# A joint mask selector, pair products in blocks of 64 tokens, and expert 0's tokens picked by one-hot matmuls

## The chip, the cores and the metric

One Trainium2 chip, one of its cores. The metric is the device time of one execution in microseconds. Three executions of the kernel before took 1454.84, 1455.51 and 1457.64 us (median 1455.51).

## The reference, cut to what matters

Two transformer blocks run one after the other on 512 tokens of width 1024, all in fp32. The change touches three places of them.

```
# first block, SSD mixer: a_cs are cumulative sums within chunks of 128 tokens
seg = a_cs[..., :, None] - a_cs[..., None, :]
lmat = exp(where(causal, seg, -inf))                       # 12 heads, 4 chunks
y_diag = einsum('bcgls,bcghls,bcsghp->bclghp', cb, lmat, xdt)

# second block, HGRN2 mixer: b is the running sum of log f within a chunk of 64 tokens
diff = b[:, :, :, None, :] - b[:, :, None, :, :]
decay = where(causal, exp(minimum(diff, 0)), 0)
scores = einsum('bhtk,bhtsk,bhsk->bhts', qc, decay, kc)    # 4 heads, 128 channels k
o_intra = einsum('bhts,bhsv->bhtv', scores, vc)

# second block, mixture of experts: top group, then top 2 of its 4 experts
for e in range(16):
    h = silu(t @ w_gate[e]) * (t @ w_up[e])                # 1024 -> 512
    y = y + gates[:, e:e + 1] * (h @ w_down[e])            # 512 -> 1024
```

## The kernel before, in words

All tokens stay on one core, in four tiles of 128 tokens. A dense product with weights is made with fp32 precision out of three matmuls of rounded operands: `split` (L265) lets ScalarE copy a weight unit to `whi` (L270) and VectorE subtract that from the raw weights into `wlo` (L271), and `mm3` (L274) issues hi times hi (L276), hi times lo (L277 or L278) and lo times hi. A plain fp32 matmul shows as two matmul records in the trace (28 groups of 4 matmuls at L1416 are 224 records). Weights come in units of 512 KB through SyncE's DMA queue (L212) into a ring of raw buffers; `fill` loads and splits ahead. Which engine subtracts a unit, and behind which instruction, is written in `s.plan` and `s.fence`. The order of each engine's instructions is set by a list scheduler from priorities; `issue_after` adds a dependence and `ahead` moves priority. Side work such as the mixers runs as generators between the dense matmuls of a neighbouring stage and shares TensorE with them.

**SSD masks.** For each of 16 units (4 chunks times 4 groups) `ssd_mask_unit` (L830) fills one PSUM bank: the causal mask (L840), the cumulative sums of three heads broadcast to all rows by a selector column, once for their high parts (L841) and once for their low parts (L842), both with 48 rows of the array, and the product of B and C (L843). ScalarE takes the exponential (L846), VectorE multiplies (L847).

**HGRN2 pair products.** `hgrn_head` (L1375) makes the scores of a head as a sum over eight groups. The diagonal is k times q masked by the identity (L1393, L1394). For each level l from 6 down to 0 the tokens are cut into blocks of 2 times 2^l, the left half of each block scaled as keys and the right half as queries (L1407 to L1412, exponential on ScalarE at L1409), and four matmuls of 128 by 128 (L1416), one for each token tile, give all pairs; VectorE copies those of this level under a mask into `PT` (L1417). Thus a head has 32 matmuls, all heads 128, or 256 records.

**Entry to the experts.** `moe` projects the mixers' output with `w_out_2`, and for each token tile `after` adds the residual (L403), transposes the tile (L2023), computes the router's logits (L2028), the rank of each token within its expert (`route_tile`, `ranks`, L1731 to L1733), and a one-hot matrix of expert 0's 96 slots (L2049). The normed tokens go to a DRAM tensor `xnd`. When the last tile is ranked, `slots_row` (L1829) turns the one-hot matrix into token numbers (`sn_v`, `sn_i`), and POOL gathers 96 rows of `xnd` with an indirect DMA (L1874). `expert_pick` transposes the rows (L1887), and `put_split` (L315) makes `ex_xh` and `ex_xl`, on which expert 0's first matmul waits. Expert 1 is fetched in the same way right behind. Two of the weight splits of this stretch are on POOL (L271). A DMA of SyncE (`mark`, L2116) stands ahead of the next weight loads; the final norm's gain is broadcast by TensorE (L125). After that each expert has 4 units of gate weights, 4 of up weights and 4 of down weights, and the tokens of expert e+1 are picked while expert e is computed.

Of the kernel before, what the change touches and what calls it, by code (L numbers as in the profile page):

```python
# [7 lines left out]
F32 = mybir.dt.float32  # L8
# [62 lines left out]
class Kern:  # L71
# [202 lines left out]
    def mm3(s, ps, a, asl, b, bsl, first, last):  # L274
# [3 lines left out]
        mm(ps, a.lo[asl], b.hi[bsl], start=False, stop=last)  # L278
# [99 lines left out]
    def projR(s, src, ld, nk, get, x, after, tail=3, mid=None, lag=2, order=None):  # L378
# [4 lines left out]
        for half in range(2):  # L383
            cs = slice(half * 512, half * 512 + 512)
# [16 lines left out]
            for tt in range(NT):  # L401
                mms(ws, tt)
                nc.vector.tensor_add(x[:, tt, cs], x[:, tt, cs], pss[tt])  # L403
# [372 lines left out]
    def ssd_dt(s, pd, x):  # L776
# [38 lines left out]
        s.ssd_sel = pd.tile([48, 16], F32R, name="ssd_sel")  # L815
        V.tensor_add(s.ssd_sel, eq[:, 3], eq[:, 2])
        hm = pd.tile([48, 3], F32, name="ssd_hm")
        V.tensor_reduce(hm, eq[:, 0:3], AX.X, OP.add)
        yield
        pt = s.ptr.tile([P, 512], F32, name="tr")  # L820
        nc.tensor.transpose(pt[:48, 0:P], cs[:, 0].rearrange("p a b -> p (a b)"), s.ident)
        hl = s.tmp.tile([48, 2, P], F32R, name="ssd_hl", tag="h")
        hi, lo = hl[:, 0], hl[:, 1]
        s.put_split(pt[:48, 0:P], hi, lo)
        s.ssd_cs = Split(*(pd.tile([48, 3, P], F32R, name="ssd_c" + i) for i in ("H", "L")))
        sh = [48, 3, P]
        for o, v in ((s.ssd_cs.hi, hi), (s.ssd_cs.lo, lo)):
            V.tensor_mul(o, v.bitcast(F32)[:, None, :].to_broadcast(sh), hm[:, :, None].to_broadcast(sh))
        yield

    def ssd_mask_unit(s, pl, c, g):
# [7 lines left out]
        sel = s.ssd_sel[:, u:u + 1].to_broadcast([48, P])  # L839
# [506 lines left out]
    def hgrn_consts(s, pool):  # L1346
# [30 lines left out]
    def hgrn_head(s, pt, h, fq, PT, kd, qx, el):  # L1377
# [950 lines left out]
```

## Time and profile before

| | |
|---|---|
| profiled execution, its own time | 1453.98 us |
| its span | 1452.2 us |
| mean granted TensorE clock | 0.987 |
| busy: TensorE, VectorE, ScalarE, POOL | 96%, 67%, 54%, 7% |
| chain that ended last, share of TensorE | 86% |
| stretch 1110 to 1120 us: TensorE busy | 8.89 of 10 us |
| stretch 1150 to 1160 us: TensorE busy | 10.0 of 10 us |

The time of an execution is a little above the span of its profile. "Busy" of TensorE counts modelled ends of pipelined matmuls, so that distances from one start to the next say more of its pace than durations. The first block's mixer lies around 60 to 260 us, the second block's around 800 to 1060, its projection up to 1119, and the experts from there to the end.

### The profile page before, as it was taken

Reading aid. Unit: us, or ns where it says so; the run is one execution under the profiler, and the core shown is the slowest. Engines: PE = TensorE matmul, PEld = TensorE weight load, DVE = VectorE, ACT = ScalarE, POOL = GpSimd, SP = SyncE. Lnnn points to the kernel's source line nnn. Section 1 sums busy time; section 2 is a strip of 40 time slices with the busy share of each in tenths; the row PEclk is TensorE's granted clock in tenths of the full one; section 3 lists DMA queues with packets and bytes.
Section 4 is the critical chain, followed back from the end, with each engine's and each line's share of the span. In section 5 each row is a group of like instructions: output and inputs, shape, how many; then the busy total and the mean of one; then the engine's idle time right before and its main releaser. Section 6 shows DMA issues by size and latency. Waiting matters only on the chain.

```text
span 1452.2 us, 20178 instructions
## 1 busy us (share of the span) xinstructions
PE 1399.7 (96%) x7467; PEld 1130.2 (78%) x7467; DVE 977.7 (67%) x1772; ACT 779.2 (54%) x1200; POOL 103.8 (7%) x103
## 2 busy tenths in 40 slices
PE   7999999999999999999999999999998599999996
PEld 6888887787879888888888889877887367777774
DVE  6989577565465444444365997766555599999997
ACT  6465654434334333233344685554443388888885
POOL 1000000010010000000000400000102111111111
PEclk9999999999999999999999999999999699999998
DMA  7353342521223333323232423120754899999993
GB/s 199 92 136 112 90 131 73 174 88 58 75 71 116 102 95 94 101 88 100 89 101 87 134 74 88 41 77 18 260 204 172 226 357 356 353 343 349 349 349 130
DMA packets 145933, 223.51 MB, mean 154 GB/s; under 512 B 18466, under 2 KB 71106, under 8 KB 145816
## 3 DMA queue, kind: packets, MB, share of 16 engines
q1 hardware_dynamic: 136852, 200.48, 42.7%
q0 software_dynamic: 3568, 10.34, 3.0%
q10 hardware_dynamic: 5412, 11.37, 2.2%
q8 instruction: 59, 0.97, 0.3%
q14 instruction: 42, 0.34, 0.1%
HBM read 208.41 MB, written 14.95 MB: 154 GB/s over the span
## 4 chain that ended last, share of the span: by engine, by line
PE 86%; DVE 6%; ACT 3%; DMA 2%; issue 2%; POOL 1%; DVEq 0%; SPq 0%; ACTq 0%; POOLq 0%
PE mm L276 24%; PE mm L278 24%; PE mm L277 24%; PE sm L1416 2%; PE tr L1548 1%; PE tr L323 1%; PE tr L1887 1%; PE sm L1532 1%; POOL rs_r L291 1%; DMA ex_g<-xnd,sn_i 1%; DVE wlo L271 1%; PE sm L879 1%; PE sm L276 1%; PE tr L1540 1%; PE sm L2028 1%
## 5 line engine op out<-in xcount | busy, mean ns | idle before, releaser
L271 DVE TENSOR_TENSOR wlo<-raw,whi 128x1024 fp32r<-128x1024 f32 (+1 forms) x351 | 423.6, 1222 | 216.4 <-ACT whi L270 213.5
L270 ACT ACTIVATE whi<-raw 128x1024 fp32r<-128x1024 f32 (+1 forms) x356 | 372.7, 1057 | 293.2 <-PE mm L277 154.0
L276 PE MATMUL mm<-hT_hi,whi 128*128 128x512 f32 (+1 forms) x768 | 283.2, 369 | 1.9 <-DVE x L403 1.7
L278 PE MATMUL mm<-hT_hi,wlo 128*128 128x512 f32 (+1 forms) x768 | 281.5, 367 | 0.0
L277 PE MATMUL mm<-hT_lo,whi 128*128 128x512 f32 (+1 forms) x768 | 280.9, 366 | 0.0
L276 PE MATMUL mm<-whi,hT_hi 128*128 128x512 f32 (+1 forms) x592 | 219.7, 371 | 1.4 <-ACT hT_hi L315 1.4
L278 PE MATMUL mm<-whi,hT_lo 128*128 128x512 f32 (+1 forms) x592 | 217.9, 368 | 0.0
L277 PE MATMUL mm<-wlo,hT_hi 128*128 128x512 f32 (+1 forms) x592 | 217.0, 367 | 0.0
L278 PEld LDWEIGHTS mm<-hT_hi,wlo 128*128 128x128 f32 x768 | 144.7, 188 | 24.3
L276 PEld LDWEIGHTS mm<-hT_hi,whi 128*128 128x128 f32 x768 | 144.3, 188 | 24.8 <-DVE x L403 1.9
L277 PEld LDWEIGHTS mm<-hT_lo,whi 128*128 128x128 f32 x768 | 144.6, 188 | 23.3
L276 PEld LDWEIGHTS mm<-whi,hT_hi 128*128 128x128 f32 x592 | 111.8, 189 | 20.7 <-ACT hT_hi L315 2.3
L278 PEld LDWEIGHTS mm<-whi,hT_lo 128*128 128x128 f32 x592 | 111.7, 189 | 19.2 <-issue 0.6
L277 PEld LDWEIGHTS mm<-wlo,hT_hi 128*128 128x128 f32 x592 | 112.0, 189 | 18.5 <-issue 1.0
L276 PE MATMUL mm<-whi,ex_xh 128*96 128x512 f32 x256 | 102.8, 402 | 1.3 <-ACT ex_xh L315 0.6
L291 POOL TENSOR_TENSOR rs_r<-rs_v,mhalf 128x1 f32<-128x1 f32 (+2 forms) x42 | 33.4, 798 | 980.2 <-DVE rs_v L289 823.9
L277 PE MATMUL mm<-wlo,ex_xh 128*96 128x512 f32 x256 | 101.4, 396 | 0.0
L278 PE MATMUL mm<-whi,ex_xl 128*96 128x512 f32 x256 | 100.9, 395 | 0.0
L276 PEld LDWEIGHTS mm<-whi,ex_xh 128*96 128x96 f32 x256 | 41.5, 162 | 19.0 <-ACT ex_xh L315 1.1
L278 PEld LDWEIGHTS mm<-whi,ex_xl 128*96 128x96 f32 x256 | 41.6, 162 | 18.1
L277 PEld LDWEIGHTS mm<-wlo,ex_xh 128*96 128x96 f32 x256 | 41.8, 163 | 16.9
L1246 DVE SCALAR_TENSOR_TENSOR cv<-mm,cols,cv 128x511 f32<-128x511 f32 (+1 forms) x44 | 33.0, 749 | 30.0 <-ACT cv L1243 29.2
(568 smaller groups left out, 2060.3 us busy)
## 6 DMA issues: line engine op xcount, KB each, us to landing
raw<-in_w_gate SPq DMA_DIRECT2D x64, 512.0 KB
raw<-in_w_up SPq DMA_DIRECT2D x64, 512.0 KB
raw<-in_w_down SPq DMA_DIRECT2D x64, 512.0 KB
raw<-in_ffn_w_up SPq DMA_DIRECT2D x44, 512.0 KB
raw<-in_w_in SPq DMA_DIRECT2D x40, 512.0 KB
raw<-in_ffn_w_down SPq DMA_DIRECT2D x22, 512.0 KB
raw<-in_w_out SPq DMA_DIRECT2D x16, 512.0 KB
raw<-in_w_in SPq DMA_DIRECT2D x8, 520.0 KB
```

The source lines that it names most:

```text
L270: s.hi_op = s.nc.scalar.activation(hv, v, AF.Copy).ins
L271: eng.tensor_sub(lv, v, hv.bitcast(F32))
L276: mm(ps, a.hi[asl], b.hi[bsl], start=first, stop=False)
L277: mm(ps, a.hi[asl], b.lo[bsl], start=False, stop=False)
L278: mm(ps, a.lo[asl], b.hi[bsl], start=False, stop=last)
L291: s.pow_op = nc.gpsimd.tensor_tensor(r, v, s.mhalf[:, :n], OP.pow).ins
L323: nc.tensor.transpose(ps[:, i * P:(i + 1) * P], src[:, (k0 + i) * P:(k0 + i + 1) * P], s.ident)
L879: nc.tensor.matmul(yd[:, o:o + 64], L[:, j], xdt[:, h], start=True, stop=True)
L1246: V.scalar_tensor_tensor(y[:, d:], ps[:, :512 - d], cw[:, w:w + 1], y[:, d:], op0=OP.mult, op1=OP.add)
L1416: nc.tensor.matmul(ps[:, sl], qk[:, sl], qk[:, sl], start=True, stop=True)
L1532: nc.tensor.matmul(ps[:, :n], qa[:, h, sl], ka[:, h, :n], start=True, stop=False)
L1540: nc.tensor.transpose(pt[:, j * P:j * P + P], p[:, j * P:j * P + P], s.ident)
```

## The change

Three parts of the program are changed.

1. The high and low parts of the cumulative sums are stacked into 128 rows (0 to 47 and 64 to 111, the rest zero by the selector), so that one matmul with 128 rows (L848) takes the place of the two with 48 rows.
2. The pair products are made for blocks of 64 tokens. Diagonal and levels 5 to 0 take eight matmuls of 64 by 64 each, whose outputs lie in PSUM partitions 0 to 63 and 64 to 127 in turn, that is in the two column halves of the array (L1413); level 6 takes four, in the lower half alone (L1442). Two levels share a PSUM bank. VectorE's masked copies are half as long (256 elements) and go into a new tile `PC`; three ScalarE copies per head bring level 6 and the blocks into `PT`. A head has 60 matmuls in 4 steps of TensorE instead of 32 in 8.
3. Expert 0's tokens are not gathered. `first` multiplies each token tile (stationary) by its one-hot matrix, now in fp32 (L2063, 8 matmuls per tile); ScalarE and VectorE read the two PSUM banks and apply the norm's gain (L2164 to L2167). Expert 1 alone is gathered, with its one-hot matrix made per tile and its pick placed after the third up unit. The two POOL splits go to VectorE, behind the residual adds; the `mark` DMA is gone; the final gain comes by a POOL DMA of 128 by 1024 instead of two broadcast matmuls.

```diff
 def ssd_mask_unit
-        nc.tensor.matmul(o, sel, s.ssd_cs.hi.rearrange("p j t -> p (j t)"), start=False, stop=False)
-        nc.tensor.matmul(o, sel, s.ssd_cs.lo.rearrange("p j t -> p (j t)"), start=False, stop=True)
+        nc.tensor.matmul(o, s.ssd_sel[:, u:u + 1].to_broadcast([P, P]), s.ssd_cs.rearrange("p j t -> p (j t)"),
+                         start=False, stop=True)
 def hgrn_head
+        PC = pt.tile([P, NT, 64], F32, name="hg_PC", bufs=2)
+        def blocks(ps, c0, a, b_):
+            for tt in range(NT):
+                for i in range(2):
+                    c = tt * P + i * 64
+                    nc.tensor.matmul(ps[i * 64:i * 64 + 64, c0 + tt * 64:c0 + tt * 64 + 64], a[:, c:c + 64],
+                                     b_[:, c:c + 64], start=True, stop=True)
...
-                nc.tensor.matmul(ps[:, sl], qk[:, sl], qk[:, sl], start=True, stop=True)
-            V.copy_predicated(PT[:, h], s.hg_mask[l][:, None, :].to_broadcast([P, NT, P]),
-                              ps.rearrange("p (a b) -> p a b", a=NT))
+            if l == 6:
+                blocks(ps, 0, k, q)
+                for tt in range(NT):
+                    nc.tensor.matmul(ps[0:64, 256 + tt * 64:320 + tt * 64], qk[:, tt * P:tt * P + 64],
+                                     qk[:, tt * P + 64:tt * P + P], start=True, stop=True)
+                V.tensor_mul(PC, pv[:, 0], s.hg_id[:, None, :].to_broadcast([P, NT, 64]))
+                nc.scalar.activation(PT[0:64, h, :, 64:], pv[0:64, 1], AF.Copy)
+            else:
+                for i, (_, v) in enumerate(qks):
+                    blocks(ps, i * 256, v, v)
+                for i, (n, _) in enumerate(qks):
+                    V.copy_predicated(PC, s.hg_mask[n][:, None, :].to_broadcast([P, NT, 64]), pv[:, i])
+        for i in range(2):
+            r = slice(i * 64, i * 64 + 64)
+            nc.scalar.activation(PT[r, h, :, r], PC[r], AF.Copy)
 def moe
+        def first(tt):
+            for b in range(2):
+                for k in range(4):
+                    c = (4 * b + k) * P
+                    nc.tensor.matmul(p0[b][:, k * CAP:(k + 1) * CAP], x[:, tt, c:c + P], oh[0][:, tt],
+                                     start=tt == 0 and k == 0, stop=tt == 3 and k == 3)
...
-            V.tensor_scalar(oh[:, tt], s.slot, s.rk[:, tt, 0:1], None, op0=OP.is_equal)
+            for e in range(2):
+                V.tensor_scalar(oh[e][:, tt], s.slot, s.rk[:, tt, e:e + 1], None, op0=OP.is_equal)
...
-        s.plan = [(nc.gpsimd, []), (nc.gpsimd, [s.pow_op])]
+        s.plan = [(V, [s.add_ops[0]]), (V, [s.add_ops[1]])]
...
-            gf = s.bcast_pe(s.gain, grow, "gain")
-        with s.tc.issue_after(nc.sync.dma_start(mark, ix[0]).ins):
-            s.fill()
-        xT = s.expert_pick(pe, xgs[0])
+        xT = s.expert_xT(pe)
+        for k in range(KD):
+            ps = p0[k // 4][:, k % 4 * CAP:k % 4 * CAP + CAP]
+            gk = s.cols2[:, 96 + k:97 + k]
+            nc.scalar.activation(xT.hi[:, k], ps, AF.Copy, scale=gk)
+            V.scalar_tensor_tensor(xT.lo[:, k], ps, gk, xT.hi[:, k].bitcast(F32), op0=OP.mult, op1=OP.subtract)
...
-            xT = s.expert_pick(pe, xgs[(e + 1) % XG])
+            with s.tc.issue_after(s.gate_op) if e == 0 else nullcontext():
+                xT = s.expert_pick(pe, xgs[(e + 1) % XG])
```

The scheduler moves instructions with it. TensorE in the second block's mixer, first head: L276 to L278 are dense matmuls of the projection, `sm` is a PSUM bank of the pair products. Before, a group of eight:

```order
L278 MATMUL mm<-hT_hi,wlo 128x512
L276 MATMUL mm<-hT_hi,whi 128x512
L277 MATMUL mm<-hT_lo,whi 128x512
L1416 MATMUL sm<-hg_qk 128x128 x8
L278 MATMUL mm<-hT_hi,wlo 128x512
```

and now, from level 6 of the first head on:

```order
L276 MATMUL mm<-hT_hi,whi 128x512
L1442 MATMUL sm<-hg_qk 64x64 x4
L277 MATMUL mm<-hT_lo,whi 128x512
L1413 MATMUL sm<-hg_qk 64x64 x8
L278 MATMUL mm<-hT_hi,wlo 128x512
L276 MATMUL mm<-hT_hi,whi 128x512
L1413 MATMUL sm<-hg_qk 64x64 x8
L277 MATMUL mm<-hT_lo,whi 128x512
L278 MATMUL mm<-hT_hi,wlo 128x512
```

The 64 by 64 matmuls stand in 33 runs in all, with full-width matmuls between them, down to runs of one in the second head.

TensorE at the entry to the experts: `tr` and `sm` with `rt_` names are the router, L2063 are the one-hot matmuls, and the rows with `ex_xh` are expert 0's gate. Before:

```order
L1748 LDWEIGHTS rt_o
L1748 MATMUL sm<-rt_Mb,rt_o 128x16
L125 MATMUL mm<-grow,ones 128x512 x2
L1887 MATMUL tr<-ident,ex_g_9992 128x96 x8
L276 MATMUL mm<-whi,ex_xh 96x512
L277 MATMUL mm<-wlo,ex_xh 96x512
```

and now, from the last dense matmul of the projection up to the last logits, and then up to the gate:

```order
L278 MATMUL mm<-whi,hT_lo 128x512
L2063 MATMUL mm<-rt_oh_9582,x 128x96 x15
L2071 MATMUL tr<-ident,x 128x128 x4
L2063 MATMUL mm<-rt_oh_9582,x 128x96
L2076 MATMUL sm<-rt_w,rt_h 128x20 x4
```

```order
L1785 MATMUL sm<-rt_Mb,rt_o 128x16
L2063 MATMUL mm<-rt_oh_9582,x 128x96 x8
L1871 LDWEIGHTS rt_oh_9583
L1871 MATMUL sm<-rt_tb,rt_oh_9583 96x2
L276 MATMUL mm<-whi,ex_xh 96x512
L277 MATMUL mm<-wlo,ex_xh 96x512
```

The gather's transposes and the broadcast are gone from here; the one-hot matmuls of tiles 0 and 1 fill TensorE behind the projection, those of tile 3 (L2063 x8) stand right ahead of the gate, and the pick of expert 1 stands behind the third up unit.

VectorE at the same place now has the low parts of expert 0's tokens (`ex_xl`) between route work and weight splits:

```order
L2167 SCALAR_TENSOR_TENSOR ex_xl<-mm,cols_2799,ex_xh 128x96 x2
L1805 TENSOR_TENSOR rt_w<-rt_w,rt_se 128x4
L1834 TENSOR_REDUCE rt_rk_10279<-rt_x 128x4
L2167 SCALAR_TENSOR_TENSOR ex_xl<-mm,cols_2799,ex_xh 128x96 x2
L1806 RECIPROCAL rt_w<-rt_w 128x4
L1833 TENSOR_TENSOR rt_x<-rt_M,rt_rk 128x64
L1807 TENSOR_TENSOR rt_w<-rt_w,rt_e_10253 128x4
L271 TENSOR_TENSOR wlo<-raw,whi 128x1024
```

Route work that stood alone while the gather was under way now shares the queue with what expert 0 waits for.

## Rows read from the trace of the kernel before

**Rows 1.** Page: the chain that ended last, share of the span by engine.

```profile
PE 86%; DVE 6%; ACT 3%; DMA 2%; issue 2%; POOL 1%; DVEq 0%; SPq 0%; ACTq 0%; POOLq 0%
```

**Rows 2.** Windows: length, busy us of PE, PEld, DVE, ACT, POOL; PEclk, DMA share, GB/s.

```profile
200.00:230.00 30.00, 30.00 (x195) 25.36 (x194) 23.60 (x43) 14.91 (x36) 1.10 (x2) 1.00 0.34 105
830.00:890.00 60.00, 60.00 (x419) 55.04 (x418) 51.29 (x106) 51.71 (x70) 0.00 (x0) 1.00 0.31 89
1120.00:1130.00 10.00, 3.70 (x26) 3.18 (x27) 8.47 (x43) 3.69 (x6) 3.25 (x3) 0.61 0.89 315
1130.00:1140.00 10.00, 4.07 (x12) 1.43 (x10) 5.21 (x24) 2.51 (x5) 3.42 (x3) 0.50 0.84 81
1200.00:1300.00 100.00, 100.00 (x480) 71.11 (x479) 92.45 (x92) 85.92 (x103) 14.16 (x12) 1.00 1.04 353
```

**Rows 3.** Timeline of PE, 16 pair-product records: start us, us to last end.

```profile
835.45 0.40 PE L277 MATMUL mm<-hT_lo,whi 128*128 128x512 f32 x1
835.68 1.95 PE L1416 MATMUL sm<-hg_qk 128*128 128x128 f32 x16
837.38 0.47 PE L278 MATMUL mm<-hT_hi,wlo 128*128 128x512 f32 x1
837.70 0.39 PE L276 MATMUL mm<-hT_hi,whi 128*128 128x512 f32 x1
```

**Rows 4.** Timeline of PE, one SSD mask unit.

```profile
173.75 0.33 PE L840 MATMUL sm<-neg_lt,identb 128*128 128x384 bf16 x1
...
174.28 0.34 PE L842 MATMUL sm<-ssd_cL,ssd_sel 48*128 48x384 f32 x1
174.55 0.49 PE L843 MATMUL sm<-CT,BT 128*128 128x128 f32 x2
174.79 0.36 PE L276 MATMUL mm<-memT_hi,whi 128*128 128x256 f32 x1
```

**Rows 5.** Timeline of PE, four records on 64 rows of the array between dense matmuls.

```profile
58.55 0.40 PE L278 MATMUL mm<-hT_hi,wlo 128*128 128x512 f32 x1
58.88 0.49 PE L597 MATMUL sm<-s_oo,s_bre 64*128 64x128 f32 x4
...
59.64 0.40 PE L277 MATMUL mm<-hT_lo,whi 128*128 128x512 f32 x1
```

**Rows 6.** Timeline of PE, 64 by 64 matmuls of the S5 mixer in column halves.

```profile
105.63 0.40 PE L278 MATMUL mm<-hT_hi,wlo 128*128 128x512 f32 x1
105.95 2.09 PE L686 MATMUL sm<-s_U,s_I 128*64 128x64 f32 x64
107.97 0.66 PE L695 MATMUL sm<-s_U,s_T 128*128 128x64 f32 x4
```

**Rows 7.** Chain of waits at the entry to the experts: start us, us, what.

```profile
1117.49 0.80 PE sm L2028 x8
...
1118.70 1.75 DVE rt_oh L2049
...
1122.77 1.90 PE sm L2028 x8
...
1124.87 1.32 DVE rs_t L301
...
1129.00 0.18 DVE rt_oh L2049
...
1130.83 14.23 DMA ex_g<-xnd,sn_i
...
1146.64 0.73 PE mm L276
```

**Rows 8.** Timeline of POOL at the same place, two weight splits.

```profile
1118.03 2.35 POOL L271 TENSOR_TENSOR wlo<-raw,whi 128x1024 fp32r<-128x1024 f32 x1 [1.13 <-ACT whi L270]
...
1123.82 2.35 POOL L271 TENSOR_TENSOR wlo<-raw,whi 128x1024 fp32r<-128x1024 f32 x1
```

**Rows 9.** Tile `ex_g`, 1120 to 1175 us: the gathers, from issue to landing.

```profile
DMA to landing us min/median/max: 8.4/11.4/14.4
```

More of the change, by code (lines that the diff above doesn't have):

```diff
@@ L277, in mm3 @@
         mm(ps, a.hi[asl], b.lo[bsl], start=False, stop=False)
-        mm(ps, a.lo[asl], b.hi[bsl], start=False, stop=last)
+        return mm(ps, a.lo[asl], b.hi[bsl], start=False, stop=last).ins
     def rstd(s, ss, n, width, pool, v0=None, out=None):
@@ L1389, in hgrn_head @@
         yield
-        ps = s.psm.tile([P, 512], F32, name="sm")
-        for tt in range(NT):
-            sl = slice(tt * P, tt * P + P)
-            nc.tensor.matmul(ps[:, sl], k[:, sl], q[:, sl], start=True, stop=True)
-        V.tensor_mul(PT[:, h], ps.rearrange("p (a b) -> p a b", a=NT), s.ident[:, None, :].to_broadcast([P, NT, P]))
-        yield
+        PC = pt.tile([P, NT, 64], F32, name="hg_PC", bufs=2)
[5 more added lines that the diff above has]
+                                     b_[:, c:c + 64], start=True, stop=True)
+        qks = []
         for l in range(6, -1, -1):
@@ L1571, in mixer2 @@
         el = ph.tile([P, 4, NT], F32, name="hg_el")
+        nc.gpsimd.memset(PT[64:P, :, :, 0:64], 0.0)
         bg = s.bg
@@ L2015, in moe @@
         s.rr = pr.tile([P, NT], F32, name="rt_r")
-        oh = pr.tile([P, NT, CAP], BF16, name="rt_oh")
+        oh = [pr.tile([P, NT, CAP], (F32, BF16)[e], name=f"rt_oh{e}") for e in range(2)]
+        p0 = []
+        def first(tt):
[4 more added lines that the diff above has]
+                                     start=tt == 0 and k == 0, stop=tt == 3 and k == 3)
         def logits(tt, half):
@@ L2060, in after @@
                     ranks(tt - 1)
+            if tt == 3:
+                p0.extend(s.pmm.tile([P, 512], F32, name="mm") for _ in range(2))
+                for i in range(3):
+                    first(i)
             V.scalar_tensor_tensor(la[:, tt], pl[:, tt * 20:tt * 20 + 20], r, s.rb, op0=OP.mult, op1=OP.add)
@@ L2076, in moe @@
         s.projR("w_out_2", D, KD, lambda half, k: mixT, x, after, mid=mid, lag=0, order=(4, 6, 0, 2), tail=3)
+        gf = s.gain.tile([P, D], F32, name="gain")
+        with s.tc.issue_after(s.pow_op):
+            nc.gpsimd.dma_start(gf, dap(A["final_norm_2"], 0, [[0, P], [1, D]]))
         ranks(3)
+        first(3)
         s.hAc.close()
@@ L2086, in moe @@
         s.release()
-        hi_op = None
-        s.plan = [(nc.gpsimd, []), (nc.gpsimd, [s.pow_op])]
+        s.plan = [(V, [s.add_ops[0]]), (V, [s.add_ops[1]])]
+        late, s.late = s.late, 1000
         s.fill(most=L3, splits=2)
-        hi_op = s.hi_op
+        s.late = late
         with s.tc.issue_after(s.last_h):
             s.fill(most=1, splits=0)
-        ix = []
-        for e in range(XG):
-            if e:
-                oh = pn.tile([P, NT, CAP], BF16, name="sn_oh")
-                sh = [P, NT, CAP]
-                V.tensor_tensor(oh, s.slot[:, None, :].to_broadcast(sh), s.rk[:, :, e:e + 1].to_broadcast(sh), OP.is_equal)
-            with s.tc.issue_after(s.rank_op):
-                ix.append(s.slots_row(pn, e, oh))
-            s.gather(xgs[e], ix[e])
-            if not e:
-                s.fence = [s.row_op]
-        grow = s.tmp.tile([1, D], F32, name="grow", tag="h", bufs=1)
-        with s.tc.issue_after(hi_op):
-            nc.scalar.dma_start(grow, dap(A["final_norm_2"], 0, [[D, 1], [1, D]]))
-        with s.tc.issue_after(s.logit_op), s.tc.issue_after(hi_op):
-            gf = s.bcast_pe(s.gain, grow, "gain")
+        with s.tc.issue_after(s.rank_op):
+            ix1 = s.slots_row(pn, 1, oh[1])
+        s.gather(xgs[1], ix1)
         for tt in range(AL, NT):
```

96 lines of the change are left out of this document (58 added, 38 removed).

## The prediction

> **What bounds the kernel now.** I read the page first: the chain that ended last lies on TensorE (PE) for 86% of the span [rows 1]. So a change is worth what it takes from TensorE's own sequence, or from the few stretches in which TensorE waits. The windows tell these apart [rows 2]. In the SSD stretch (200 to 230 us) and in the HGRN2 stretch (830 to 890 us) TensorE is busy for all of the window, while VectorE has 23.6 of 30 and 51.3 of 60 us and ScalarE 14.9 of 30 and 51.7 of 60: there the pace of matmuls is the time. From 1120 to 1140 us TensorE is busy for 3.70 and 4.07 of 10 us, with a granted clock of 0.61 and 0.50 of full speed (0.50 is the level of 1.2 GHz, 1.00 that of 2.4): there a chain of small steps and one transfer is the time. In the steady experts (1200 to 1300 us) TensorE is full, VectorE 92%, and the DMA runs at 353 GB/s with a share of 1.04, so hardly anything is spare there.
>
> Durations of pipelined matmuls overlap, so I use distances between starts. A dense matmul with 512 moving columns goes by every 0.23 us (835.45 to 835.68), and the run of 16 pair-product records with both its neighbours takes 1.70 us plus 0.32 - 0.23 us of the matmul behind it, that is 0.112 us per record [rows 3].
>
> **1. SSD masks.** A unit takes from 173.75 to 174.79, 1.04 us, for three matmuls of 384 columns and two records of the product of B and C [rows 4]. By the pace of rows 3 a matmul of 384 columns is worth 0.23 x 384/512 = 0.17 us and a record 0.11 us, which gives 3 x 0.17 + 2 x 0.11 = 0.73 us: 0.31 us are lost where the array goes from 128 rows to 48 and back. The same loss shows elsewhere: four records on 64 rows between dense matmuls take from 58.55 to 59.64, 1.09 us [rows 5]; less two dense ones (0.46) that is 0.63 us, for 0.22 us of work if the two row halves run at once (0.41 us lost), and 0.45 us if they do not (0.18 us lost). The joint matmul has 128 rows, so the unit should fall to 2 x 0.17 + 2 x 0.11 = 0.56 us: 0.48 us less, 16 units, **-7.7 us**. The least is the removed L842 alone, 174.28 to 174.55, 0.27 x 16 = 4.3 us. Should the whole gain show, TensorE's 30 us of the window become some 27, still above VectorE's 23.6 [rows 2], so nothing else is late first. The new steps ahead (a memset, two copies, a full transpose in the constants) are a few instructions on engines with room there: nothing.
>
> **2. HGRN2 pair products.** Before: 256 records x 0.112 = 28.7 us [rows 3]. After: 240 matmuls of 64 by 64. The row that is nearest is the S5 mixer's, whose 32 matmuls have the same shape and alternate between the column halves: 64 records from 105.95 to 107.97 [rows 6], 2.02/32 = 0.063 us per matmul, of which some is the exit. I take 0.06 us for the 216 in both halves (13.0 us) and 0.12 us for the 24 that have no partner next to them (16 of level 6 and 8 that the order leaves alone, 2.8 us): 15.8 us. But each run of them stands between full-width matmuls, and rows 6 show the price of the border as well: 0.32 us from the dense matmul to the first record where 0.23 is usual, and a second loss on the way out. By the order there are 33 such runs. With rows 5's bounds for a way in and out, 0.18 and 0.41 us, and 0.33 us taken (nearer to the upper end, because the SSD unit of rows 4 lost 0.31): 33 x 0.33 = 10.9 us. Sum 26.7, so **-2 us** (from -7 at 0.18 us to +0.6 at 0.41 us).
>
> The Trainium skill (TensorEngine Tiling (Array Packing), Theoretical Speedup) puts the gain of two column tiles at up to 2x; the same page (Key Properties) says that a change of the tiling mode drains the engine. By the first alone this part would give half of TensorE's pair products back, by the second it depends on how often the mode changes; the trace has a price for that border and the order has 33 of them, which is why I keep little.
>
> VectorE saves 4 of 28 masked copies and half of the length of the rest, ScalarE gets 12 copies of up to 256 columns; at 51.7 of 60 us [rows 2] it can take them as long as TensorE's stretch shrinks by no more than a few us. Nothing for both, and up to +2 us if ScalarE's cover is gone.
>
> **3. Entry to the experts.** The chain [rows 7] goes from the logits of tile 2 (1117.49) through the logits of tile 3 (1122.77, 1.90 us) and the ranks to the last one-hot matrix (1129.00), then 14.23 us in the gather, and reaches expert 0's gate at 1146.64. What falls out:
> - The gather, its index work, the transposes and the split of their result: all from 1129.2 to 1146.6, 17.4 us.
> - The two POOL splits of 2.35 us [rows 8] lie exactly beside two VectorE steps that take 1.75 and 1.32 us [rows 7]; the same one-hot step takes 0.18 us at 1129.00. On VectorE the splits stand elsewhere: 2.7 us back, of which I take 2, since VectorE now does that work.
> - The logits at full clock take 0.80 instead of 1.90 us [rows 7], if the one-hot matmuls of tiles 0 and 1 (16 x 2 records) fill the hole behind the projection and hold the clock: 1 us. The first 3 us of the gate, at half clock before, give 1 us more.
>
> What comes in: one-hot matmuls of tiles 2 and 3, 16 x 2 records x 0.11 = 3.5 us, of which tile 2's lies partly beside VectorE's ranking; I count 3. The low and high parts of the tokens, some 0.4 us each on ScalarE and VectorE, of which the first ones delay the gate: 1 us. Two one-hot matrices per tile instead of one: 0.5 us. VectorE's route work, which ran beside the gather before, now shares its queue with expert 0's low parts and weight splits: 5.2 us of it from 1130 to 1140 [rows 2] and, as an estimate, 3 us more behind, of which I count 3 us as stalls of TensorE and the rest as absorbed by the units that are already split. Sum: 17.4 + 2 + 2 - 3 - 1 - 0.5 - 3 = **-14 us**. Bounds: without any of the 4 us that I credit to clock and POOL, and with twice the VectorE stalls, -7; with the stalls hidden, -17. Expert 1's gather is issued about when the gate starts, and its pick stands 24 gate and 18 up matmuls of 0.23 us behind that, 9.7 us; landing took 8.4 to 14.4 us [rows 9], so from nothing to 5 us of wait, inside these bounds. The gain's DMA and the missing `mark` are off the path: nothing.
>
> **Sum.** -7.7 - 2 - 14 = -23.7 us against the profiled execution of 1453.98 us: 1430.3. That execution was 1.5 us below the median of 1455.51, so for the median I say **1432 us** (1431.8).
>
> **The rivals.**
> - *Column halves cost a full record each* (ends slower). If a 64 by 64 fp32 matmul took two records at the pace of the 64-column matmuls with a full-width stationary right behind the S5 ones (L695, four records in 0.66 us, about 0.11 each), part 2 would take 240 x 0.22 + 10.9 = 63.7 instead of 28.7 us, +35, and the kernel 1453.98 - 7.7 + 35 - 14, about 1467 us. It decides from (28.7 + 21.7 - 10.9)/240 = 0.165 us per matmul on. Against it: rows 6, the same shape at 0.063. 3 in 100.
> - *The border is free.* If a run of 64 by 64 matmuls loses nothing at its ends, part 2 gives 15.8 - 28.7, about -13 us, and the kernel is at 1421 us. That is what the Trainium skill (TensorEngine Tiling (Array Packing), Theoretical Speedup) would lead one to expect. For it: the runs are short and some borders may hide behind dense matmuls. Against it: rows 5 and 6, and rows 4. 10 in 100.
> - *The time moves behind the entry.* Expert 0 starts early, but VectorE (already 92% in the steady experts) and the weight stream at 353 GB/s cannot follow an earlier start, or the slow transfers of 1130 to 1140 (81 GB/s at a share of 0.84) stay and hold up expert 1's rows and the weights: 8 us of part 3 are given back, 1440 us. For it: rows 2. Against it: the ring of raw buffers is full when the experts start. 17 in 100.
> - *The masks keep their loss*, because the border lay in the bf16 mask matmul L840 or in the selector's load and not in the 48 rows: part 1 gives 4.3 us, 1435 us. 10 in 100.
>
> **How the numbers follow.** The forecast as summed has 58 in 100, the rivals 3, 10, 17 and 10, and 2 are left for a mishap that costs more than all gains. The range reaches from the free border with a little more at the entry, 1420, to the time moved behind the entry with the losses of part 2, 1442; about 15 in 100 lie outside. A difference of 0.2% (2.9 us) is about the least that a measurement of this kernel can tell from none. All cases but the first rival and the mishap lie far below 1452.6, so faster 0.94, same 0.02, slower 0.04.
>
> **What would show it.** Right: a unit of masks takes about 0.56 us from L840 to behind L843; records of L1413 start in pairs about 0.06 us apart, and each of their runs has a gap of 0.1 us ahead and a larger one behind; the first matmul on `ex_xh` starts 16 to 19 us earlier behind the last dense matmul of the projection than now, with a granted clock of 1.0 from 1120 to 1140. Wrong: a stretch 830 to 948 that shrinks by 10 us or grows; a gate that waits for VectorE's splits longer than 3 us; waits of TensorE for raw weights near the end.

## The result and the profile after

The changed kernel takes **1433.3 us** (median of four executions, 1430.94 to 1436.72) against 1455.32 us before: a ratio of 0.9847, 95% interval 0.9823 to 0.9871, or 22.0 us less. The forecast of 1432 us with its range of 1420 to 1442 held. The profiled execution took 1434.49 us, 19.5 less than the profiled one before.

The page of the kernel after, the chain that ended last by engine (as [rows 1]):

```profile
PE 85%; DVE 7%; ACT 3%; issue 2%; POOL 1%; DMA 1%; DVEq 0%; SPq 0%; POOLq 0%; ACTq 0%
```

TensorE still holds the chain, and the share of DMA is down from 2% to 1%: the gather has left it. To see where the 19.5 us come from, I compare the start of the n-th dense matmul of L276 in both traces; there are 1888 in each, in the same order.

| the n-th L276 matmul | before, us | after, us | after - before |
|---|---|---|---|
| 241st, SSD begins | 174.79 | 175.25 | +0.46 |
| 361st, SSD over | 277.18 | 268.72 | -8.46 |
| 1441st, HGRN2 over | 1061.61 | 1054.06 | -7.55 |
| first of expert 0's gate | 1146.63 | 1125.54 | -21.1 |
| last one | 1433.45 | 1413.44 | -20.0 |

Just before HGRN2, at 817 us, the difference is still -8.44. So the SSD part brought 8.9 us, the pair products cost 0.9, and the entry brought 13.5 at the gate, of which 1.1 went back by the end. The forecast had -7.7, -2 and -14.

The last dense matmul of the projection, from which the distance to the gate is measured below, in the trace of before and then of after:

```profile
1118.50 0.40 PE L278 MATMUL mm<-whi,hT_lo 128*128 128x512 f32 x1
```

```profile
1111.00 0.39 PE L278 MATMUL mm<-whi,hT_lo 128*128 128x512 f32 x1
```

Windows of the kernel after (columns as in [rows 2]):

```profile
830.00:890.00 60.00, 59.36 (x511) 50.60 (x508) 43.60 (x102) 49.91 (x72) 0.00 (x0) 0.94 0.26 72
866.00:868.00 2.00, 2.00 (x13) 1.34 (x12) 0.92 (x1) 1.97 (x3) 0.00 (x0) 1.00 0.00 0
868.00:870.00 2.00, 2.00 (x21) 1.53 (x20) 1.28 (x4) 1.97 (x3) 0.00 (x0) 0.62 0.00 0
870.00:872.00 2.00, 2.00 (x9) 1.54 (x9) 1.72 (x6) 0.89 (x2) 0.00 (x0) 0.50 0.03 8
872.00:874.00 2.00, 2.00 (x11) 2.00 (x10) 0.76 (x2) 1.43 (x4) 0.00 (x0) 0.50 0.00 0
874.00:876.00 2.00, 2.00 (x14) 2.00 (x13) 0.00 (x0) 1.97 (x3) 0.00 (x0) 0.68 0.00 0
1110.00:1120.00 10.00, 8.91 (x68) 8.48 (x67) 8.06 (x44) 3.91 (x7) 1.13 (x2) 0.88 1.00 323
1120.00:1130.00 10.00, 9.22 (x45) 7.63 (x45) 5.48 (x29) 3.20 (x9) 1.06 (x1) 0.61 0.92 328
1130.00:1140.00 10.00, 10.00 (x55) 6.97 (x54) 9.84 (x27) 7.61 (x9) 2.11 (x1) 1.00 1.02 346
...
1200.00:1300.00 100.00, 100.00 (x478) 71.14 (x477) 92.20 (x92) 85.90 (x103) 13.80 (x11) 1.00 1.04 352
```

The entry is filled: TensorE is busy for 9.22 and 10.0 us where it had 3.70 and 4.07 [rows 2]. The steady experts are as before. Two places were not foreseen. From 868 to 876 us TensorE works at the 1.2 GHz level for most of the time (0.62, 0.50, 0.50, 0.68), which costs 2 x 0.38 + 4 x 0.50 + 2 x 0.32 = 3.4 us of full-speed work; and from 1120 to 1130 the granted clock is 0.61, where I had said 1.0.

Waits of TensorE in the kernel after from 1111 to 1160 us (engine and line, what it waited for: us in total, times, longest), in the place of the 14.23 us of the gather in [rows 7]:

```profile
PE mm L276 <- ACT ex_xh L315: 1.5, 1, 1.5
PE mm L276 <- ACT ex_xh L2166: 0.7, 1, 0.7
PE mm L2063 <- DVE rt_oh L2098: 0.6, 1, 0.6
PE sm L2076 <- ACT rt_h L2073: 0.5, 1, 0.5
```

The longest is for expert 1's tokens (L315), behind the pick; no wait is left that ends on a gather's landing, though the gathers still land only after 7.3 to 12.1 us, against 8.4 to 14.4 before [rows 9].

One SSD mask unit of the kernel after, timeline of TensorE (as [rows 4]; L848 is the causal mask, and the joint matmul is L849, not L848 as the description of the change has it):

```profile
174.77 0.33 PE L848 MATMUL sm<-neg_lt,identb 128*128 128x384 bf16 x1
174.80 0.47 PE L849 MATMUL sm<-ssd_cH,ssd_sel 128*128 128x384 f32 x1
175.10 0.38 PE L851 MATMUL sm<-CT,BT 128*128 128x128 f32 x2
175.25 0.36 PE L276 MATMUL mm<-memT_hi,whi 128*128 128x256 f32 x1
```

The unit takes 0.48 us, 0.56 less than the 1.04 before (I had said 0.56 long, 0.48 less), and 16 x 0.56 = 9.0 us is the stretch's gain. The two matmuls of 384 columns take 174.77 to 175.10, 0.33 us, as summed; it is the product's two records, with 0.15 us up to the next dense matmul, that I had too dear at 0.22.

Pair products of the kernel after, timeline of TensorE: a run of eight matmuls (16 records), then matmuls standing alone between dense ones.

```profile
860.36 0.69 PE L1413 MATMUL sm<-hg_qk 128*64 128x64 f32 x16
860.97 0.39 PE L278 MATMUL mm<-whi,hT_lo 128*128 128x260 f32 x1
861.29 0.69 PE L1413 MATMUL sm<-hg_qk 128*64 128x64 f32 x16
...
864.85 0.33 PE L1413 MATMUL sm<-hg_q,hg_k 128*64 128x64 f32 x2
865.10 0.39 PE L278 MATMUL mm<-whi,hT_lo 128*128 128x260 f32 x1
865.42 0.33 PE L1413 MATMUL sm<-hg_q,hg_k 128*64 128x64 f32 x2
```

A dense matmul of 260 columns is worth 0.12 us here. A run of eight with one dense matmul takes 861.29 - 860.36 = 0.93 us: 0.12 + 8 x 0.06 + 0.33. A single one with its dense matmul takes 865.42 - 864.85 = 0.57: 0.12 + 0.12 + 0.33. With 0.06 us for a paired matmul and 0.12 us for one that stands alone, as in the forecast, the loss per run is 0.33 us in both, so it is the same for a run of eight as for a run of one.

### The profile page after: what moved, and what is told of

It reads as the page before. It is cut to its first block, busy times and chain, and to the rows that moved or that the text cites. A ratio compares the mean times of both kernels' runs of the same rounds, so it can differ in the third digit from the quotient of the medians.

```text
span 1432.5 us, 20693 instructions
## 1 busy us (share of the span) xinstructions
PE 1395.2 (97%) x7723; PEld 1129.5 (79%) x7723; DVE 966.3 (67%) x1782; ACT 781.6 (55%) x1214; POOL 100.1 (7%) x105
## 4 chain that ended last, share of the span: by engine, by line
PE 85%; DVE 7%; ACT 3%; issue 2%; POOL 1%; DMA 1%; DVEq 0%; SPq 0%; POOLq 0%; ACTq 0%
PE mm L276 24%; PE mm L278 24%; PE mm L277 24%; PE sm L1413 1%; PE tr L1584 1%; PE tr L323 1%; PE tr L1921 1%; PE sm L1568 1%; POOL rs_r L291 1%; DVE wlo L271 1%; PE mm L2063 1%; PE sm L887 1%; DVE cv L1032 1%; PE sm L276 1%; PE tr L1576 1%
## 5 line engine op out<-in xcount | busy, mean ns | idle before, releaser
L276 PE MATMUL mm<-hT_hi,whi 128*128 128x512 f32 (+1 forms) x768 | 284.1, 370 | 1.9 <-DVE x L404 1.6
L278 PE MATMUL mm<-hT_hi,wlo 128*128 128x512 f32 (+1 forms) x768 | 281.4, 367 | 0.0
L276 PE MATMUL mm<-whi,hT_hi 128*128 128x512 f32 (+1 forms) x592 | 220.9, 373 | 1.4 <-ACT hT_hi L315 1.4
L278 PE MATMUL mm<-whi,hT_lo 128*128 128x512 f32 (+1 forms) x592 | 219.5, 371 | 0.0
L278 PEld LDWEIGHTS mm<-hT_hi,wlo 128*128 128x128 f32 x768 | 144.7, 188 | 25.1
L276 PEld LDWEIGHTS mm<-hT_hi,whi 128*128 128x128 f32 x768 | 144.3, 188 | 25.2 <-DVE x L404 1.8
L276 PEld LDWEIGHTS mm<-whi,hT_hi 128*128 128x128 f32 x592 | 113.1, 191 | 20.6 <-ACT hT_hi L315 2.3
L278 PEld LDWEIGHTS mm<-whi,hT_lo 128*128 128x128 f32 x592 | 113.1, 191 | 19.6 <-issue 0.8
L276 PE MATMUL mm<-whi,ex_xh 128*96 128x512 f32 x256 | 102.8, 401 | 2.1 <-ACT ex_xh L315 1.5
L278 PE MATMUL mm<-whi,ex_xl 128*96 128x512 f32 x256 | 101.3, 396 | 0.0
L276 PEld LDWEIGHTS mm<-whi,ex_xh 128*96 128x96 f32 x256 | 41.7, 163 | 19.4 <-ACT ex_xh L315 1.6
L278 PEld LDWEIGHTS mm<-whi,ex_xl 128*96 128x96 f32 x256 | 41.6, 162 | 18.6 <-DVE ex_xl L315 0.3
```

Source lines behind the costliest of these rows:

```text
L276: mm(ps, a.hi[asl], b.hi[bsl], start=first, stop=False)
L278: return mm(ps, a.lo[asl], b.hi[bsl], start=False, stop=last).ins
```

## The experiments

The theory after the result: the masks are worth their border (9 us), the pair products lose at 33 borders what they save, and the entry lacks some 3 us of its gain, to the clock or to another wait.

**The three parts alone.** Each was put into the kernel before by itself. First the masks:

```diff
-        nc.tensor.matmul(o, sel, s.ssd_cs.hi.rearrange("p j t -> p (j t)"), start=False, stop=False)
-        nc.tensor.matmul(o, sel, s.ssd_cs.lo.rearrange("p j t -> p (j t)"), start=False, stop=True)
+        nc.tensor.matmul(o, s.ssd_sel[:, u:u + 1].to_broadcast([P, P]), s.ssd_cs.rearrange("p j t -> p (j t)"),
+                         start=False, stop=True)
```

> The kernel before with part 1 alone (joint selector of 128 rows). Theory (the borders between 48-row and 128-row matmuls are what is saved): 8 to 9 us faster than before, all of it between 173 and 256 us. Rival (only the removed matmul L842 is saved): 4.3 us faster.

1447.42 us, ratio 0.9941 (0.9924 to 0.9957). In the traces, the 241st dense matmul starts 1.80 us later than before and the 361st 7.18 earlier: 9.0 us in the SSD stretch, and nothing after it. This is 16 units of 0.56 us, not the 4.3 us of the removed matmul alone: the loss went with the 48 rows.

Then the pair products:

```diff
+        def blocks(ps, c0, a, b_):
...
-                nc.tensor.matmul(ps[:, sl], qk[:, sl], qk[:, sl], start=True, stop=True)
+                for i, (_, v) in enumerate(qks):
+                    blocks(ps, i * 256, v, v)
```

> The kernel before with part 2 alone (pair products in blocks of 64). Theory (33 borders and a stretch at half clock eat the saved matmul time): within 2 us of before, with a stretch of granted clock 0.5 in the HGRN2 stretch where single 64 by 64 matmuls alternate with dense ones. Rival (the halves pay, and the loss seen in the changed kernel comes from what stands around it): 8 us or more faster. Second rival (ScalarE or VectorE has become the bound): the same time as before, with TensorE idle between its runs and no half clock.

1453.22 us, ratio 0.9982 (0.9972 to 0.9992), 2.6 us less by the ratio: neither the half clock of the theory nor the 8 us of the rival. From the 1200th dense matmul of L276 (825 us in the kernel before, ahead of the first pair product) to the 1441st this kernel gains 3.1 us (+2.73 to -0.41), with the same 0.93 and 0.57 us per run and the full clock. Ahead of that, before its first pair product at 835.77 us, it lost 1.7 us (+1.01 to +2.73) to a spell of lower clock, so that counted from 779 us the stretch is only 1.4 us shorter (windows of this kernel):

```profile
806.00:814.00 8.00, 6.77 (x33) 6.48 (x34) 7.23 (x19) 5.87 (x11) 1.07 (x2) 0.57 0.76 237
...
870.00:880.00 10.00, 10.00 (x109) 7.90 (x105) 6.97 (x15) 8.21 (x12) 0.00 (x0) 1.00 0.38 104
```

And the entry:

```diff
-            V.tensor_scalar(oh[:, tt], s.slot, s.rk[:, tt, 0:1], None, op0=OP.is_equal)
+            for e in range(2):
+                V.tensor_scalar(oh[e][:, tt], s.slot, s.rk[:, tt, e:e + 1], None, op0=OP.is_equal)
...
+                for i in range(3):
+                    first(i)
...
-        s.plan = [(nc.gpsimd, []), (nc.gpsimd, [s.pow_op])]
+        s.plan = [(V, [s.add_ops[0]]), (V, [s.add_ops[1]])]
```

> The kernel before with part 3 alone (expert 0 by one-hot matmuls). Theory: 12 us faster, the same as the changed kernel shows between the last dense matmul of the projection and the third expert. Rival (the experts catch up with the weight stream when they start early): 6 us or less.

1442.7 us, ratio 0.9915 (0.9898 to 0.9932). In its trace 14.0 us fall out between the projection and the end. By the ratios the three parts give 8.6, 2.6 and 12.4 us, together 23.6, where the whole change gave 22: they add up within what is measured.

**The change without the pair products.**

```diff
-                for i, (_, v) in enumerate(qks):
-                    blocks(ps, i * 256, v, v)
+            for tt in range(NT):
+                sl = slice(tt * P, tt * P + P)
+                nc.tensor.matmul(ps[:, sl], qk[:, sl], qk[:, sl], start=True, stop=True)
```

> The changed kernel with part 2 undone (pair products 128 by 128 as before). Theory: 0 to 2 us faster than the changed kernel, that is 22 to 24 us faster than before, and no half clock between 820 and 950 us. Rival (part 2 is worth its matmul time): 8 us or more slower than the changed kernel.

1433.54 us, ratio 0.9843 (0.9826 to 0.9859), the same as with them; the rival falls, and the clock stayed at 1.00 from 820 to 950 us. It shows something else as well: its order at the entry is that of the change, but the clock held until the gate had started, and fell behind that. Timelines of TensorE, this kernel first (L2034 are the one-hot matmuls of tiles 2 and 3), then the change (L2063), and two windows of this kernel:

```profile
1118.01 2.02 PE L2034 MATMUL mm<-rt_oh,x 128*128 128x96 f32 x16 [0.60 <-DVE rt_oh L2069]
...
1120.71 2.02 PE L2034 MATMUL mm<-rt_oh,x 128*128 128x96 f32 x16
...
1124.49 0.47 PE L276 MATMUL mm<-whi,ex_xh 128*96 128x512 f32 x1 [1.76 <-ACT ex_xh L2137]
```

```profile
1117.57 3.70 PE L2063 MATMUL mm<-rt_oh,x 128*128 128x96 f32 x16 [0.60 <-DVE rt_oh L2098]
...
1121.95 3.73 PE L2063 MATMUL mm<-rt_oh,x 128*128 128x96 f32 x16
...
1125.54 0.72 PE L276 MATMUL mm<-whi,ex_xh 128*96 128x512 f32 x1
```

```profile
1118.00:1126.00 8.00, 5.63 (x48) 4.68 (x48) 4.68 (x34) 1.81 (x6) 0.00 (x0) 1.00 1.04 409
1126.00:1130.00 4.00, 3.90 (x11) 2.24 (x11) 3.68 (x16) 2.44 (x6) 1.06 (x1) 0.57 1.05 388
```

Behind the last dense matmul of the projection the gate starts after 13.05 us here and after 14.54 in the change, 28.13 before. At the lower clock the two groups take 3.4 us longer together, yet the gate comes only 1.5 us later, because at the full clock it waits 1.76 us for `ex_xh`. So the clock covers a second wait.

**Fewer borders.** Two runs per pair of levels are made into one: a head matmul that depends on what is ready last, and the others behind it.

```diff
-                for i, (_, v) in enumerate(qks):
-                    blocks(ps, i * 256, v, v)
+                with s.ahead(500):
+                    v = qks[1][1]
+                    head = block(ps, 256, v, v, 0)
+                    with s.tc.issue_after(head.ins):
...
```

> The changed kernel with the same pair products in 16 runs instead of 33: in each PSUM bank one matmul of the level that is ready last goes first and the other 11 or 15 follow right behind it. Theory (each run costs about 0.33 us at its ends): 17 x 0.33 = 5.6 us faster than the changed kernel, up to 3 us more where the stretch at half clock does not come, 1425 to 1428 us. Rival (VectorE or ScalarE sets the pace of the HGRN2 stretch): no faster than the changed kernel, 1433 us, with TensorE idle ahead of its runs.

1430.54 us, ratio 0.9821 (0.9805 to 0.9837), short of the theory. From the 1200th dense matmul of L276 to the 1441st this kernel gains 5.3 us on the kernel before (-7.63 to -12.90); with 33 runs the pair products alone gained 3.1 at the same full clock. So 17 runs fewer gave 2.1 us of the 17 x 0.33 = 5.6. What is missing shows as idle time: from 820 to 960 us TensorE is busy for 134.8 of 140 us here, and for 139.0 with the pair products alone. The larger part lies in the second window of this kernel:

```profile
820.00:850.00 30.00, 30.00 (x248) 24.78 (x247) 25.39 (x54) 29.16 (x38) 0.00 (x0) 1.00 0.32 90
...
850.00:870.00 20.00, 17.07 (x213) 15.51 (x212) 17.53 (x43) 19.74 (x30) 0.00 (x0) 1.00 0.30 81
```

TensorE idles 2.9 us in the second window, while ScalarE is busy for 29.16 of 30 and 19.74 of 20 us. The waits that end TensorE's idle time are for VectorE's `hg_qk` and `hg_E`, which stand around ScalarE's exponentials, so that I take ScalarE for the next bound; that was argued, not shown.

The half clock near 870 us was not gone with the single matmuls. Of the six kernels with joined runs, four show a spell of it between 867 and 878 us in their profiled execution, this one not; in the kernel whose store is moved (below):

```profile
868.00:872.00 4.00, 4.00 (x22) 4.00 (x23) 2.60 (x8) 3.96 (x7) 0.00 (x0) 0.59 0.02 4
```

**The clock at the entry.** The one-hot matmuls of tiles 1 and 2 are kept back until the last logits, so that the logits come earlier.

```diff
-                for i in range(3):
-                    first(i)
+                first(0)
+                with s.tc.issue_after(o):
+                    first(1)
+                    first(2)
```

> The changed kernel with the one-hot matmuls of tiles 1 and 2 queued behind the router's logits of tile 3 instead of ahead of the transposes of tile 3. Theory (TensorE's holes at 1115 to 1117.5 us let the clock fall, and the chain waits for 16 records that it does not need): logits of tile 3 some 1.7 us earlier, the one-hot matmuls of tiles 2 and 3 at full clock (3.7 us less) or part of it, so 2 to 5 us faster than the changed kernel, 1428 to 1431 us. Rival (VectorE's route work and the weight splits set the pace behind the entry): the gate starts earlier, but the third expert does not, 1433 us.

1432.01 us, ratio 0.9828 (0.9812 to 0.9845). The one-hot matmuls run at the full clock, and the gate waits all the longer: it stands 13.42 us behind the projection, 1.1 less than in the change, of which 0.6 is left at the end. The timeline of TensorE, the chain of waits, and the first steps of ScalarE and VectorE behind the wait in this kernel:

```profile
1117.78 2.02 PE L2063 MATMUL mm<-rt_oh,x 128*128 128x96 f32 x16
...
1122.32 0.47 PE L276 MATMUL mm<-whi,ex_xh 128*96 128x512 f32 x1 [2.52 <-ACT ex_xh L2168]
```

```profile
1111.83 9.99 DMA xnd<-hl
1121.94 0.29 DVE rt_y L1819
```

```profile
1121.93 0.34 ACT L2168 ACTIVATE ex_xh<-mm,cols 128x96 fp32r<-128x96 f32 x1 [4.87 <-DMA raw<-in_w_up]
1121.94 0.29 DVE L1819 TENSOR_TENSOR rt_y<-rt_tb,rt_M 128x128 bf16<-128x128 bf16 x1 [3.92 <-DMA xnd<-hl]
```

The chain now runs through the store of the last normed tile (`hl`) to `xnd`, 10 us under way, to VectorE's first route step (`rt_y`), which is written behind it. ScalarE's first `ex_xh`, for which the gate waits, is held for several things at once; its row names the last of them by the profile, a weight load, in this kernel and in the change. But it starts in the same moment as `rt_y`, and 0.10 to 0.11 us behind the last update that the store's semaphore shows, in the traces of all seven kernels in which the store is on SyncE's queue and the one-hot matmuls are done by then. So the next wait at this place is that store. With both edits:

```diff
+                with s.tc.issue_after(o):
+                    first(1)
+                    first(2)
...
+                    head = block(ps, 256, v, v, 0)
```

> e5_runs and e6_first together. Theory: the gains add, 1420 to 1426 us. Rival (one of them is given back later, in the weight stream): no faster than the better one of the two.

1431.18 us, ratio 0.9824 (0.9808 to 0.984): not faster than with fewer borders alone, so the gains did not add in the time; the trace has the shorter HGRN2 stretch and 0.7 us of the entry. The same order of the one-hot matmuls without the pair products:

```diff
-                for i, (_, v) in enumerate(qks):
-                    blocks(ps, i * 256, v, v)
...
+                with s.tc.issue_after(o):
+                    first(1)
+                    first(2)
```

> The changed kernel with part 2 undone and the order of e6_first. Theory: 2 to 5 us faster than e4_no_pairs (1433.5 us), and slower than e7_both by 5 us, what the pair products save in long runs. Rival (the pair products save nothing in any order): the same as e7_both.

1438.19 us, ratio 0.986 (0.9835 to 0.9885). The time decides between neither theory nor rival. The gate stands 12.79 us behind the projection, against 13.05 without the new order, and from the projection to the end this kernel takes 1.0 us less than that one, not 2 to 5. The loss lies at 150 us, in the S5 mixer, which no edit here touches. Windows of this kernel, then of the change:

```profile
150.00:155.00 5.00, 5.00 (x35) 4.65 (x35) 3.02 (x9) 1.15 (x2) 0.83 (x2) 0.50 0.00 0
155.00:160.00 5.00, 5.00 (x39) 4.55 (x39) 1.03 (x1) 0.49 (x1) 0.00 (x0) 0.50 0.00 0
```

```profile
150.00:155.00 5.00, 4.88 (x66) 4.44 (x66) 3.03 (x11) 1.16 (x3) 1.04 (x2) 1.00 0.00 0
155.00:160.00 5.00, 5.00 (x48) 4.93 (x47) 3.33 (x3) 3.37 (x5) 0.00 (x0) 1.00 0.60 152
```

Ten microseconds at half clock are 5 us lost; the 241st dense matmul starts 5.65 us later than before, against 0.46 in the change. Three of its executions took 1438.05 to 1438.72 us at mean clocks of 0.989 and 0.990, the fourth 1432.67 at 0.995.

**The store.** First it is put on another queue:

```diff
-                s.last_h = nc.sync.dma_start(s.xnd[tt * P:(tt + 1) * P, :], hs[tt]).ins
+                s.last_h = nc.gpsimd.dma_start(s.xnd[tt * P:(tt + 1) * P, :], hs[tt]).ins
```

> e7_both with the last store of normed tokens (xnd<-hl, 512 KB) issued by POOL on its own queue instead of by SyncE behind weight loads. Theory (with the clock kept, expert 0's first split and VectorE's route work wait for this store, 10 us from issue to landing, because their buffers lie where its source lay): landing within 7 us, the gate 2 to 3 us earlier behind the last dense matmul, 1428 to 1429 us. Rival (the store is slow because all DMA engines are taken, whatever the queue): landing and gate as in e7_both, 1431 us.

1430.57 us, ratio 0.9822 (0.9805 to 0.984). The store in the trace of this kernel (tile `xnd`: the issue, who waited, the time to landing), and then, with both edits and the store on SyncE's queue, its issue and the step that starts when it has landed:

```profile
L2115 POOL DMA_DIRECT2D xnd<-hl x1: 600/600/600, 1111.1 to 1111.1; - x1
...
  ACT ex_xh L2180: 4.5, 1
...
DMA to landing us min/median/max: 9.4/9.4/9.4
```

```profile
L2115 SPq DMA_DIRECT2D xnd<-hl x1: 338/338/338, 1109.6 to 1109.6; - x1
...
1119.71 0.29 DVE L1831 TENSOR_TENSOR rt_y<-rt_tb,rt_M 128x128 bf16<-128x128 bf16 x1 [3.91 <-DMA xnd<-hl]
```

9.4 us on POOL's queue, issued 0.6 us later behind the projection, against 10.0 on SyncE's: it lands 12.9 us behind the last dense matmul in both, and the gate stands 13.46 us behind it against 13.42. So what delays it is not the queue. The DMA share in the windows of the change is 1.00, 0.92 and 1.02 from 1110 to 1140, so the engines behind the queues are taken. The Trainium skill (DMA: Bandwidth & Descriptors, Issuing engines are not separate DMA queues) says that transfers of different issuing engines end up on the same 16 DMA engines; the two landing times of 12.9 us agree. The rows also name the waiting instruction, now the store's own: ScalarE's `ex_xh`, 4.5 us.

**ScalarE's share.** The copies of the blocks go to POOL, alone and with the store:

```diff
-            nc.scalar.activation(PT[r, h, :, r], PC[r], AF.Copy)
+            nc.gpsimd.tensor_copy(PT[r, h, :, r], PC[r])
```

> e5_runs with the eight copies of PC into PT on POOL instead of ScalarE. Theory (with few runs ScalarE is the bound of the HGRN2 stretch, 19.7 of 20 us busy from 850 to 870 while TensorE is idle for 2.9): TensorE idle for 1 us less or more, 1 to 3 us faster than e5_runs. Rival (a POOL copy beside VectorE slows VectorE's steps, as the two POOL splits did before): no faster, VectorE steps of 0.4 us that take over 1 us.

```diff
-            nc.scalar.activation(PT[r, h, :, r], PC[r], AF.Copy)
+            nc.gpsimd.tensor_copy(PT[r, h, :, r], PC[r])
...
+                s.last_h = nc.gpsimd.dma_start(s.xnd[tt * P:(tt + 1) * P, :], hs[tt]).ins
```

> e9_row_store and e10_pool_copy together: the faster of the two, or 1 to 3 us below it if the two gains are of different stretches, 1426 to 1429 us.

1431.08 us, ratio 0.9835 (0.9814 to 0.9857), and 1430.7 us, ratio 0.9833 (0.9806 to 0.986). Neither differs from its counterpart with ScalarE's copies by more than the intervals. TensorE is idle for 2.88 of the 20 us from 850 to 870 in the first of them, where it was 2.93, and waits for the same two tiles; VectorE's masked copies take 0.45 us as before. So the eight copies are not what TensorE waits for there, and VectorE is not slowed either; since ScalarE is still busy for 19.59 of these 20 us, whether it is the bound stays open.

**An own place for expert 0's tokens.** `ex_xh` and `ex_xl` get a pool that nothing else uses; the ring of weight buffers is cut to make room, and the routing is put behind the last low part.

```diff
-N4 = 3
+N4 = 4
...
-N2 = 19
+N2 = 17
...
+        px = s.pool("ex0", ctx=c)
+        x0 = s.expert_xT(px)
...
-        s.route(pr, pe, lgg, lge)
+        with s.tc.issue_after(low):
+            s.route(pr, pe, lgg, lge)
```

> e7_both with buffers of their own for expert 0's tokens (ex_xh, ex_xl), one raw buffer fewer in the ring (29 for 30), and the route work queued behind expert 0's low parts on VectorE. Theory (after the clock, the landing of xnd<-hl is what the gate waits for, because these buffers lie where its source lay): the wait of ex_xh for a DMA is gone, the gate starts right behind the one-hot matmuls of tile 3 and 2 us earlier than in e7_both, 1428 to 1429 us. Rival (the weight splits and the route work set the pace of experts 0 and 1 whenever the gate starts): the gate is earlier, the second expert is not, 1431 us or more.

1436.42 us, ratio 0.9866 (0.984 to 0.9892). The gate's wait is gone, but a new one comes. What the first `ex_xh` waited for (tile `ex_xh`, 1110 to 1123 us), timeline of TensorE, chain of waits and window of this kernel:

```profile
  PE mm L2075: 5.8, 1
```

```profile
1121.05 2.02 PE L2075 MATMUL mm<-rt_oh,x 128*128 128x96 f32 x16
...
1122.94 0.46 PE L276 MATMUL mm<-whi,ex_xh 128*96 128x512 f32 x1
```

```profile
1145.50 11.06 DMA ex_g<-xnd,sn_ix
```

```profile
1145.00:1155.00 10.00, 5.20 (x25) 3.42 (x23) 7.36 (x12) 6.84 (x8) 6.83 (x2) 0.93 1.04 354
```

The gate starts 10.84 us behind the projection, without a wait, 2.6 us sooner than with both edits (13.42). ScalarE's `ex_xh` now waits for the one-hot matmuls (L2075) alone. So the 2.5 us were the place of `ex_xh`, which stood where the store still read. But the routing came so late that the next gather was issued only at 1145.50, and TensorE idled for 4.8 of 10 us there. Between the 1521st and the 1561st dense matmul 9.8 us went back. And this execution had the half clock at 150 us too. That the place made the wait is shown; what the smaller ring and the later routing cost each was not told apart, and the version is no gain.

## Why the prediction was right, point by point

- **SSD masks, -7.7 forecast, -8.9 measured** (-9.0 alone). The 48 rows were the price, as [rows 4] and [rows 5] had it: 0.56 us less per unit is 0.17 for the matmul that went and 0.39 lost with the 48 rows, where I had 0.31. The unit came out at 0.48 instead of 0.56 us; the 0.17 us for each 384-column matmul was right, and the 0.22 us for the product's two records was too dear. The rival that the masks keep their loss falls.
- **Pair products, -2 forecast, +0.9 in the profiled execution.** Its 3.4 us at the lower clock are in that; without them it is -2.5. In the two runs with the same pair products and the full clock there it is, counted from 825 us, -3.1 (alone) and -2.9 (with the one-hot matmuls kept back, -6.74 to -9.65). By the ratios it is -2.6 alone and nothing on top of the other parts. Both unit prices were right, 0.06 and 0.33 us. What failed is that all records were taken at the full clock. Near 870 us the clock fell in the profiled executions of five of the nine kernels with the new pair products, and in none of the five with the old; the kernel without them ran at mean clocks of 0.993 to 0.995, the change at 0.989 to 0.995, and its one execution at 0.995 took 1430.94 us, 2.6 less than the median of that kernel, or 1.6 with each against its own runs of the kernel before. So the clock seems to take back what the matmuls save; that the one brings the other is not shown. The rivals of a full record per column half (+35) and of a free border (-13) both fall to the rows of 860 to 866 us. The Trainium skill (TensorEngine Tiling (Array Packing), Theoretical Speedup and Key Properties) states both the gain of up to 2x and the drain at a change of mode. These rows agree with the second: 33 runs at 0.33 us are 10.9 us.
- **Entry, -14 forecast, -12.5 measured, by errors that nearly cancel.** My items up to the gate summed to 17.4 + 2 + 2 - 3 - 1 - 0.5 = 16.9 us, and I announced 16 to 19; it was 28.13 - 14.54 = 13.6. The step that failed is "hold the clock": it fell to 0.61 in the window from 1120 to 1130, and 1.5 us at the gate went with it. And a wait was missing from the sum: expert 0's tokens were placed where the store of the last tile still read, 1.8 to 2.5 us. 13.6 + 1.5 + 1.8 = 16.9; with an own place it was 28.13 - 10.84 = 17.3. On the other side I took 3 us for stalls behind the gate, and only 1.1 went back, with 1.5 us of waiting for expert 1's tokens. The order of instructions does not show a buffer that is reused; the profile before did not show this wait because the gather stood in front of it.
- **The time moves behind the entry** (1440 us): not so in the change, where the steady experts look as before. When the routing was put late it did come to pass, by way of the next gather.
- **Sum.** -8.9 + 0.9 - 12.5 and +0.5 before the SSD stretch give -20.0 in the trace; the forecast had -23.7. The median moved by 22.0. That it came within 1.3 us of the forecast is in part luck: the masks gave 1.2 us more, and the clock took some of the pair products and of the entry. The four executions of the change spread from 1430.94 at a mean clock of 0.995 to 1436.72 at 0.989, so that the profiled one, at 0.991, lies above the median.

The fastest versions are those with fewer borders, 1430.54 us, and with the store moved besides, 1430.57; both ratios overlap with that of the change (0.9805 to 0.9837 against 0.9823 to 0.9871). The shorter HGRN2 stretch is in the trace; in the time it is not certain.

## What to carry to other kernels

Price a matmul that uses part of the array by its borders first: here each run of smaller tiles between full ones cost 0.33 us whatever its length, so that stacking rows to 128 paid in full, while splitting columns in 33 runs saved some 3 us of matmul time and nothing that the whole change's time shows; joining the runs added 2 us in the trace. When a long transfer is taken out of a chain, ask what lies in the memory that its successor will write, and which store still reads it; that wait was hidden behind the transfer. And a single profiled execution can hold a spell of lower clock that the next one has not: compare windows of the clock, at the start of a stretch too, before explaining 2 to 5 us by the order of work.

## What the runs showed of the hardware

- A spell of half clock stands at one place in one profiled execution and not in another: near 870 us in five of the nine kernels with the new pair products; around 800 to 813 us in several of the experiments and neither in the kernel before nor in the change; at 150 us in two of the experiments, in one of which no edit touches that place. At the entry it began at 1117.6 us in the change, ahead of the gate, and in the same order without the pair products only at 1126.6, behind the gate's start. TensorE was busy for all of the 2 us before the fall at 868, with single matmuls and changes of mode; ahead of the one near 1118 stand waits of 0.49 and 0.60 us, and the same two stand in the kernel whose clock held there. What decides was not found.
- The loss at a change of mode, 0.33 us, is the same for a run of one matmul in one column half and of eight in both; for the 48 rows it was 0.39 us a unit.
- A store of 512 KB behind a full stream of weights landed after some 9 to 10 us, and with both edits at the same 12.9 us behind the projection from either queue.
